# Sums of weight blocks made ahead and kept in DRAM, rotary angles on GpSimd, a scaling on ScalarE

## The chip, the cores and the metric

The kernel runs on one core of one Trainium2 chip. The time is the device time of one launch in microseconds. Engines are named as in the profile: PE (TensorE matmul), PEld (its weight load), DVE (VectorE), ACT (ScalarE), POOL (GpSimd), SP (SyncE, which here issues loads). Lines are those of the kernel before, unless "after" stands beside them.

## The reference

A trunk of two decoder layers, batch 1, 1024 tokens of width 1024, all in fp32. `cond = silu(c)`; each layer multiplies it with a 1024 x 6144 matrix and gets six vectors of shift, scale and gate.

```python
def sqrelu_mlp(h, w1, w2):                      # w1 1024 x 4096, w2 4096 x 1024
    return jnp.square(jax.nn.relu(h @ w1)) @ w2

for l in range(2):
    ada = cond @ ada_w[l] + ada_b[l]
    sh1, sc1, g1, sh2, sc2, g2 = jnp.split(ada, 6, axis=-1)
    h = modulate(rmsnorm(x, norm_g[l, 0]), sh1, sc1)
    if l == 0:
        y = mlstm_mixer(h, ...)                 # 8 heads, chunks of 128 tokens
    else:
        if shared_kv is None:                   # from x, with a modulation of its own
            shared_kv = mla_shared_kv(x, kv_shift, kv_scale, kv_norm_g, kv_w_a, ..., cos, sin)
        y = mla_mixer(h, b_w_q_a, ..., cos, sin)
    x = x + g1[:, None, :] * rmsnorm(y, norm_g[l, 1])
    h = modulate(rmsnorm(x, norm_g[l, 2]), sh2, sc2)
    y = sqrelu_mlp(h, mlp_w1[l], mlp_w2[l])
    x = x + g2[:, None, :] * rmsnorm(y, norm_g[l, 3])
```

`cos` and `sin` are the rotary tables of `positions * inv_freq`. `kv_w_a` and `b_w_q_a` are the matrices that lead to the latents of layer 1.

## The kernel before

**Matmuls.** fp32 products are made of three matmuls in a reduced format (`mm3`, L243 to L246): hi x hi, hi x lo, lo x hi. Each weight tile of 128 x 1024 is therefore loaded into one of four buffers (`raw`, by SP) and split (`wsplit`): ACT copies the high part (`wh`, L202), DVE subtracts it (`wl`, L203). There are eight such halves (`ws`). Modulation vectors are made on DVE, not on PE: eight multiply-adds per 512 columns (`ada_chunk`, L346 and L348), then four transposes on PE (L328) and a reduction (L330).

**Halves of the tokens, and the MLP.** The tokens are worked on as two halves of 512. The two halves of an MLP's up product are combined so that seven products of blocks stand for eight: `w1` is cut into 16 pairs `p_` (128 columns `p_` and 128 columns `p_ + 16`, as tiles a and b of 128 x 1024; `_l` and `_r` are the upper and lower 512 rows). `Mlp` makes three sweeps over them:
- the first (`first`, L947) multiplies a's two halves with the first token half, and POOL stores one product (`m`, L967);
- the second (`second`, L973) loads a and b, forms four block sums on DVE, o_l = b_l + b_r (L990), b_l = a_l - b_l (L991), a_l = o_l - a_l (L992), o_r = a_r - a_l (L997), splits a_l by hand (`wv`, L994 on ACT and L995 on DVE) and the tile b by `wsplit`; o is stored by POOL in `s` (L998) and partial products in `u` (L1017);
- the third (`third`, L1036) loads `s` and `u` and makes the second token half's products.

Between them the down products (`up_cols`) load `w2`, and in the first sweep POOL stores its low parts (`lo`, L1156).

**Work beside the MLP of layer 0.** `two_streams` walks the sweeps as the dense stream and takes five steps of a background (`bg_latent`) per dense step: the rest of the modulation vectors, then `rope_tables`, then `latent_weights`. `rope_tables` makes per half of the positions an angle in 128 x 512: a cast (L1263), three DVE operations (L1264 to L1266), and seven multiply-adds that take away multiples of two pi (L1268); then a clamp (L1270) and what the sine on ACT needs (L1273, L1275, L1276). `latent_weights` takes six tiles of the latents' matrices: eight multiply-adds for the shift's part (L1341, L1343), a multiplication of the whole tile with the scale (L1346, DVE, 128 x 1024), `wsplit`, and stores of both parts by POOL (`lw`, L1351 and L1353); later a transpose (L1356).

**Order.** The program is written as generators that are woven into one another (`weave`, `weave_n`, `with_bg`: so many steps of the second per step of the first) and scheduled when it is built: a planner with a timeline of its own places each instruction in its engine's queue, `tc.high_priority` and `tc.issue_after` shift it. On the chip each engine runs its queue in order and waits on semaphores. SP issues most loads in its queue's order, POOL most stores.

**The start and the mixer of layer 0.** The first 45 us transpose x and make the first modulation vectors; the last weights for them (`Piece`, L2001 to L2052) use all eight `hd` buffers (128 x 1024). Then for token half 0: `gates_in`, `qk_last`, `v_in` woven with `intra0`, `og0`; for half 1: `gates_in`, and `main` (queries, keys, values) woven with `intra0` of that half (L2294). `bgs` runs modulation chunks beside them. `k4` is a pool of 24 tiles (4 KB per partition) that the mixer and the MLP share.

Of the kernel before, what the change touches and what calls it, by code (L numbers as in the profile page):

```python
# [9 lines left out]
F32 = mybir.dt.float32  # L10
F32R = mybir.dt.float32r
# [71 lines left out]
def kernel(  # L83
# [48 lines left out]
    def raw(dt=F32):  # L132
        return sb.tile([P, 1024], dt, tag="raw", bufs=RAW, name=f"raw_{next(uid)}")
# [4 lines left out]
    def tmc(dt=F32):  # L138
        return sb.tile([P, 512], dt, tag="tmc", bufs=TMC, name=f"tmc_{next(uid)}")
# [22 lines left out]
    def scratch(shape, name):  # L162
        return dr.tile(shape, F32, tag=name, bufs=1, name=name)
# [194 lines left out]
    def ada_part(l, part):  # L358
        for j in (2 * part, 2 * part + 1):
            yield from ada_chunk(  # L360
                ada_w[l], j * 512, col(AB + l * 48 + j * 4, 4), ada[:, l, ts(j, 4)]
            )
# [553 lines left out]
                yield n7 if k == KD - 1 else n3  # L916


    NPR = DFF // P // 2
    AHEAD = 2  # L920

    class Mlp:
# [3 lines left out]
        def __init__(self, l, rows):  # L926
            self.w1, self.w2, self.rows = mlp_w1[l], mlp_w2[l], rows
            self.m = scratch([NPR, P, H], f"m{l}")
            self.u = scratch([NPR, P, 2 * H], f"u{l}")
            self.s = scratch([NPR, P, 2 * H], f"s{l}")  # L930
            self.keep = scratch([D, H], f"keep{l}")
            self.lo = scratch([4, P, DFF // P, 256], f"lo{l}")
            self.hids, self.started, self.held = ({}, {}), set(), {}
# [42 lines left out]
        def second(self, p_, ops):  # L976

            def load():  # L980
                r = [raw(), raw()]
                for i in range(2):
                    nc.sync.dma_start(
# [5 lines left out]
                l_, r_ = slice(0, 512), slice(512, 1024)  # L989
                nc.vector.tensor_add(o[:, l_], r[1][:, l_], r[1][:, r_])  # L990
                nc.vector.tensor_sub(r[1][:, l_], r[0][:, l_], r[1][:, l_])  # L991
                nc.vector.tensor_sub(r[0][:, l_], o[:, l_], r[0][:, l_])  # L992
# [33 lines left out]
        def third(self, p_, ops, buf):  # L1026


            def load():
                r, u = raw(), buf()  # L1030
                nc.sync.dma_start(r, self.s[p_])
                for i in range(2):
                    nc.sync.dma_start(u[i], self.u[p_][:, ts(i, 512)])
                return wsplit(r, 1024), u
# [216 lines left out]
    def rope_tables():  # L1251
# [7 lines left out]
        for n in range(2):  # L1259
            pi = tmc(I32)  # L1260
            nc.sync.dma_start(pi, positions[0:1, ts(n, 512)].to_broadcast([P, 512]))
            a, kf = tmc(), tmc()
            nc.vector.tensor_copy(a, pi)  # L1263
            nc.vector.tensor_scalar(a, a, inv, None, ALU.mult)  # L1264
            nc.vector.tensor_scalar(kf, a, 1.0 / (2.0 * PI), MAGIC, ALU.mult, ALU.add)
            nc.vector.tensor_scalar_add(kf, kf, -MAGIC)  # L1266
            for part in TWO_PI_PARTS:
                nc.vector.scalar_tensor_tensor(a, kf, -part, a, ALU.mult, ALU.add)  # L1268
                yield
            nc.vector.tensor_scalar(a, a, 3.1415925, -3.1415925, ALU.min, ALU.max)  # L1270
            s, t = tmc(), tmc()
# [55 lines left out]
    def latent_weights():  # L1327
# [4 lines left out]
        for b, vs in enumerate(views):  # L1332
# [7 lines left out]
            with paced():  # L1340
                nc.vector.tensor_scalar(acc, r[:, 0], sh[:, 0:1], None, ALU.mult)  # L1341
                for k in range(1, KD):
                    nc.vector.scalar_tensor_tensor(  # L1343
                        acc, r[:, k], sh[:, k : k + 1], acc, ALU.mult, ALU.add
                    )
            nc.vector.tensor_mul(r, r, A.unsqueeze(2).to_broadcast([P, KD, P]))  # L1346
            for i, t in enumerate(wsplit(r_, D)):
                if b == 2:

# [885 lines left out]
    def chain(*gs):  # L2235
        for g in gs:
            yield from g() if callable(g) else g

    bg0 = chain(*[ada_part(0, p_) for p_ in (G1, SH2, SC2, G2)])
    bg1 = chain(*[ada_kv(p_) for p_ in (0, 1)], *[ada_part(1, p_) for p_ in (SH1, SC1)])  # L2240

# [352 lines left out]
```

## Time and profile before

| what | us |
|---|---|
| median of 3 runs (lowest, highest) | 2380.63 (2376.16, 2381.13) |
| the profiled execution, whole time | 2383.9 |
| its span | 2382.1 |
| PE busy in it | 2285.4 |
| DVE busy in it | 1676.6 |
| POOL busy in it | 93.2 |

The profile is of one execution; its span runs from the first to the last recorded event, and its whole time is 1.8 us longer and 3.3 us above the median of the runs. Busy times are sums of an engine's instructions; waiting and issuing DMAs are not busy. "a <- b" behind an idle time names what ended it. The granted clock is the share of full speed at which TensorE was allowed to run. By stage, the trace has the start and the mixer of layer 0 up to about 470 us, the first sweep of its MLP to about 655, the second to about 870, and the second sweep of layer 1's MLP around 1875 to 2070.

### The profile page before, as it was taken

Reading aid. Unit: us, or ns where it says so; the run is one execution under the profiler, and the core shown is the slowest. Engines: PE = TensorE matmul, PEld = TensorE weight load, DVE = VectorE, ACT = ScalarE, POOL = GpSimd, SP = SyncE. Lnnn points to the kernel's source line nnn. Section 1 sums busy time; section 2 is a strip of 40 time slices with the busy share of each in tenths; the row PEclk is TensorE's granted clock in tenths of the full one; section 3 lists DMA queues with packets and bytes.
Section 4 is the critical chain, followed back from the end, with each engine's and each line's share of the span. In section 5 each row is a group of like instructions: output and inputs, shape, how many; then the busy total and the mean of one; then the engine's idle time right before and its main releaser. Section 6 shows DMA issues by size and latency. Waiting matters only on the chain.

```text
span 2382.1 us, 31220 instructions
## 1 busy us (share of the span) xinstructions
PE 2285.4 (96%) x11274; PEld 1886.2 (79%) x11274; DVE 1676.6 (70%) x2745; ACT 1084.1 (46%) x1811; POOL 93.2 (4%) x235
## 2 busy tenths in 40 slices
PE   8999999999898899999999989999899799999998
PEld 6888888887776788778878767878788688878887
DVE  6666767789888777767764687656638866766556
ACT  4364335674332335544444454534446233454433
POOL 1000000010011110000000000000000000000000
PEclk9999999999999999999999999999999899999999
DMA  9544454667898887655674765945256587675321
GB/s 320 162 142 118 152 155 144 196 211 250 290 295 265 282 294 252 207 191 176 203 239 159 265 218 171 327 163 184 93 149 221 157 273 228 222 252 193 115 90 70
DMA packets 402299, 482.04 MB, mean 202 GB/s; under 512 B 28419, under 2 KB 274240, under 8 KB 402144
## 3 DMA queue, kind: packets, MB, share of 16 engines
q1 hardware_dynamic: 383872, 415.44, 54.1%
q0 software_dynamic: 18272, 64.60, 7.7%
q8 instruction: 89, 1.46, 0.3%
q14 instruction: 66, 0.54, 0.1%
HBM read 358.33 MB, written 121.63 MB: 201 GB/s over the span
## 4 chain that ended last, share of the span: by engine, by line
PE 67%; issue 15%; DVE 7%; DMA 6%; ACT 2%; POOL 2%; SPq 1%; POOLq 0%; DVEq 0%; ACTq 0%
PE ps L245 11%; PE ps L244 11%; PE ps L246 11%; PE pm L244 7%; PE pm L245 7%; PE pm L246 7%; DMA raw<-in_mlp_w_dram 3%; PE pc L245 1%; PE pc L246 1%; PE pc L244 1%; DMA raw<-s 1%; PE pc L1646 1%; PE pm L791 1%; PE pm L1545 1%; DVE wl L203 1%
## 5 line engine op out<-in xcount | busy, mean ns | idle before, releaser
L202 ACT CAST wh<-raw 128x1024 fp32r<-128x1024 f32 (+4 forms) x307 | 310.6, 1015 | 508.1 <-PE pm L245 144.6
L203 DVE TENSOR_TENSOR wl<-raw,wh 128x1024 fp32r<-128x1024 f32 (+4 forms) x307 | 360.5, 1176 | 226.8 <-ACT wh L202 189.2
L244 PE MATMUL ps<-k,wh 128*128 128x512 f32 x1100 | 438.3, 399 | 8.5 <-ACT tmp L938 3.4
L245 PE MATMUL ps<-k,wh 128*128 128x512 f32 x1100 | 432.2, 393 | 2.8 <-DVE k L458 2.8
L246 PE MATMUL ps<-k,wl 128*128 128x512 f32 x1100 | 431.9, 393 | 0.8 <-DVE wl L203 0.8
L244 PEld LDWEIGHTS ps<-k,wh 128*128 128x128 f32 x1100 | 208.4, 189 | 57.2 <-ACT tmp L938 3.6
L245 PEld LDWEIGHTS ps<-k,wh 128*128 128x128 f32 x1100 | 208.6, 190 | 47.3 <-DVE k L458 4.4
L246 PEld LDWEIGHTS ps<-k,wl 128*128 128x128 f32 x1100 | 208.5, 190 | 45.6 <-DVE wl L203 1.7
L246 PE MATMUL pm<-wh,hd 128*128 128x512 f32 x488 | 191.2, 392 | 7.2 <-DVE hd L458 7.2
L244 PE MATMUL pm<-wh,hd 128*128 128x512 f32 x488 | 191.9, 393 | 1.6 <-ACT k L215 0.9
L211 DVE TENSOR_TENSOR k<-k,pm 128x512 f32<-128x512 f32 (+1 forms) x170 | 141.1, 857 | 71.8 <-PE pm L246 71.8
L245 PE MATMUL pm<-wl,hd 128*128 128x512 f32 x488 | 190.7, 391 | 0.0
L348 DVE SCALAR_TENSOR_TENSOR tma<-raw,cond,tma 128x512 f32<-128x512 f32 x168 | 125.4, 746 | 19.0 <-DMA raw<-in_ada_w_dram 10.5
L246 PEld LDWEIGHTS pm<-wh,hd 128*128 128x128 f32 x488 | 92.1, 189 | 27.4 <-DVE hd L458 8.1
L244 PEld LDWEIGHTS pm<-wh,hd 128*128 128x128 f32 x488 | 92.2, 189 | 21.8 <-ACT k L215 1.7
L245 PEld LDWEIGHTS pm<-wl,hd 128*128 128x128 f32 x488 | 92.0, 189 | 19.1 <-issue 0.2
L938 ACT ACTIVATE tmp<-tmp 128x512 f32<-128x512 f32 x80 | 50.4, 630 | 122.1 <-DVE tmp L211 102.7
L244 PE MATMUL pm<-hd,wk 128*128 128x512 f32 x256 | 101.7, 397 | 0.3 <-ACT hd L457 0.3
L244 PE MATMUL pm<-hd,wh 128*128 128x512 f32 x256 | 99.6, 390 | 1.6 <-DVE k L211 1.6
L245 PE MATMUL pm<-hd,wk 128*128 128x512 f32 x256 | 100.3, 392 | 0.6 <-DVE hd L458 0.6
L246 PE MATMUL pm<-hd,wl 128*128 128x512 f32 x256 | 99.8, 390 | 0.3 <-DVE wl L203 0.3
L246 PE MATMUL pm<-hd,wk 128*128 128x512 f32 x256 | 99.8, 390 | 0.0
(450 smaller groups left out, 4743.6 us busy)
## 6 DMA issues: line engine op xcount, KB each, us to landing
raw<-in_mlp_w_dram SPq DMA_DIRECT2D x156, 512.0 KB, 4.6
raw<-in_ada_w_dram SPq DMA_DIRECT2D x80, 512.0 KB, 4.8
raw<-in_mlp_w_dram SPq DMA_DIRECT2D x136, 256.0 KB, 4.5
raw<-in_a_w_in_dram SPq DMA_DIRECT2D x44, 512.0 KB, 4.2
lo<-wl POOLq DMA_DIRECT2D x32, 512.0 KB, 6.7
s<-k POOLq DMA_DIRECT2D x32, 512.0 KB, 4.0
u<-k POOLq DMA_DIRECT2D x32, 512.0 KB, 5.0
raw<-s SPq DMA_DIRECT2D x32, 512.0 KB, 3.6
```

Source lines behind the costliest of these rows:

```text
L202: nc.scalar.copy(hi[:, :n], r[:, :n])
L203: i = nc.vector.tensor_sub(lo[:, :n], r[:, :n], hi[:, :n].bitcast(F32))
L211: return f(*a, **k)
L244: nc.tensor.matmul(o, lh, rh, start=start, stop=False)
L245: nc.tensor.matmul(o, lh, rl, start=False, stop=False)
L246: pe_last[0] = nc.tensor.matmul(o, ll, rh, start=False, stop=stop)
L348: nc.vector.scalar_tensor_tensor(acc, r[:, kk], cond[:, k : k + 1], acc, ALU.mult, ALU.add)
L791: nc.tensor.matmul(nvs[q][:, r, i], hf.PT[p_][:, r, cs], v[2 * p_ + r], start=g == 0, stop=True,)
L938: nc.scalar.activation(s, s, AF.Relu)
L1545: nc.tensor.matmul(o[:, :w], qh, kh, start=False, stop=True)
L1646: nc.tensor.transpose(pt[:, ts(e, P)], u.prs[i][:, ts(b0 + e, P)], ident)
```

## The change

Three things change, all in layer 0 or in what runs beside its MLP.

- **Block sums.** A new generator, `block_sums`, goes over the pairs in `order` (odd ones first, then even ones, cut at 16, so all of them). Per pair POOL issues two loads of 512 KB (a and b), DVE makes the four sums in place, and POOL issues two stores of 512 KB into a new scratch in DRAM, `t0`. The first five pairs take their tiles from `hd` and run beside `gates_in` and `qk_last` of token half 0; then the tiles come from `k4`: one more pair ahead of `v_in`, and further ones at 0.2 steps per step of `main` of the second half. What is left is run to its end behind that (the `print` line). In `second`, a pair that is made loads a_l and b_l from `t0` (256 KB each), the lower half of its columns of `w1` (256 KB) and `m`, and needs no sums and no store of `s`; `third` loads its two halves from `t0`. Layer 1 keeps the old path.
- **Rotary angles.** The cast, the three operations and the seven multiply-adds move from DVE to POOL, each multiply-add as a multiplication into a third tile `d` and an addition: 18 operations per half. The clamp and what follows stay on DVE and ACT.
- **Latents' weights.** The multiplication of the tile with the scale moves from DVE (one of 128 x 1024) to ACT (eight of 128 x 128, in place).

```diff
 class Mlp:
+            self.made = not l and order or []
 def second / load():
+                if p_ in self.made:
+                    r = [raw(), raw()]
+                    nc.sync.dma_start(r[0][:, l_], t0[p_][:, 0:512])
+                    nc.sync.dma_start(r[1][:, l_], t0[p_][:, 1024:1536])
+                    nc.sync.dma_start(
+                        r[1][:, r_].rearrange("p (a b) -> p a b", b=P),
+                        wcols(self.w1, (p_ + NPR) * P, P, 4, 4),
+                    )
+                    u = k4()[:, :1024]
+                    nc.sync.dma_start(u[:, :512], self.m[p_])
+                    t = sb.tile([P, 1024], F32R, tag="ws", bufs=WS, name=f"wv_{next(uid)}")
+                    nc.scalar.copy(t[:, l_], r[0][:, l_])
+                    nc.vector.tensor_sub(t[:, r_], r[0][:, l_], t[:, l_].bitcast(F32))
+                    return (t[:, l_], t[:, r_]), wsplit(r[1], 1024), u
 def third / load():
-                nc.sync.dma_start(r, self.s[p_])
+                if p_ in self.made:
+                    nc.sync.dma_start(r[:, 0:512], t0[p_][:, 1536:2048])
+                    nc.sync.dma_start(r[:, 512:1024], t0[p_][:, 512:1024])
+                else:
+                    nc.sync.dma_start(r, self.s[p_])
 def rope_tables():
-            a, kf = tmc(), tmc()
-            nc.vector.tensor_copy(a, pi)
-            nc.vector.tensor_scalar(a, a, inv, None, ALU.mult)
-            nc.vector.tensor_scalar(kf, a, 1.0 / (2.0 * PI), MAGIC, ALU.mult, ALU.add)
-            nc.vector.tensor_scalar_add(kf, kf, -MAGIC)
+            a, kf, d = tmc(), tmc(), tmc()
+            nc.gpsimd.tensor_copy(a, pi)
+            nc.gpsimd.tensor_scalar(a, a, inv, None, ALU.mult)
+            nc.gpsimd.tensor_scalar(kf, a, 1.0 / (2.0 * PI), MAGIC, ALU.mult, ALU.add)
+            nc.gpsimd.tensor_scalar_add(kf, kf, -MAGIC)
             for part in TWO_PI_PARTS:
-                nc.vector.scalar_tensor_tensor(a, kf, -part, a, ALU.mult, ALU.add)
+                nc.gpsimd.tensor_scalar(d, kf, -part, None, ALU.mult)
+                nc.gpsimd.tensor_add(a, a, d)
                 yield
 def latent_weights():
-            nc.vector.tensor_mul(r, r, A.unsqueeze(2).to_broadcast([P, KD, P]))
+            for k in range(KD):
+                nc.scalar.activation(r[:, k], r[:, k], AF.Identity, scale=A[:, k : k + 1])
 main program
+    t0 = scratch([NPR, P, 4 * H], "t0")
+    at_prep = [k4]
+    order = [*range(1, NPR, 2), *range(0, NPR, 2)][:16]
+    def block_sums():
+        for p_ in order:
+            a, b = (at_prep[0]()[:, :1024] for _ in range(2))
+            for i, t in enumerate((a, b)):
+                nc.gpsimd.dma_start(
+                    t.rearrange("p (a b) -> p a b", b=P), wcols(mlp_w1[0], (p_ + NPR * i) * P)
+                )
+            yield
+            l_, r_ = slice(0, 512), slice(512, 1024)
+            nc.vector.tensor_add(b[:, r_], b[:, l_], b[:, r_])
+            nc.vector.tensor_sub(b[:, l_], a[:, l_], b[:, l_])
+            nc.gpsimd.dma_start(t0[p_][:, 1024:2048], b)
+            nc.vector.tensor_sub(a[:, l_], b[:, r_], a[:, l_])
+            nc.vector.tensor_sub(a[:, r_], a[:, r_], a[:, l_])
+            nc.gpsimd.dma_start(t0[p_][:, 0:1024], a)
+            yield
-    drain(with_bg(gates_in(hfs[0]), bgs, 1))
-    drain(with_bg(qk_last(hfs[0]), bgs, 1))
+    pre = block_sums()
+    at_prep[0] = hd
+    drain(with_bg(with_bg(gates_in(hfs[0]), bgs, 1), pre, 1))
+    drain(with_bg(with_bg(qk_last(hfs[0]), bgs, 1), pre, 1))
     x1 = load_x1()
+    at_prep[0] = k4
+    for _ in range(2):
+        next(pre, None)
...
-    drain(weave_n(with_bg(main, bgs, 1.5), intra0(hfs[1]), 0.95))
+    drain(weave_n(with_bg(with_bg(main, bgs, 1.5), pre, 0.2), intra0(hfs[1]), 0.95))
+    print('LEFT',len(list(pre)))
```

More of the change, by code (lines that the diff above doesn't have):

```diff
@@ L916, in residual @@
                 yield n7 if k == KD - 1 else n3
-    NPR = DFF // P // 2
     AHEAD = 2
@@ L988, in load @@
                 nc.sync.dma_start(u[:, :512], self.m[p_])
-                l_, r_ = slice(0, 512), slice(512, 1024)
                 nc.vector.tensor_add(o[:, l_], r[1][:, l_], r[1][:, r_])
@@ L2237, in chain @@
             yield from g() if callable(g) else g
+    NPR = DFF // P // 2
+    t0 = scratch([NPR, P, 4 * H], "t0")
[9 more added lines that the diff above has]
+            yield
+            l_, r_ = slice(0, 512), slice(512, 1024)
+            nc.vector.tensor_add(b[:, r_], b[:, l_], b[:, r_])
[5 more added lines that the diff above has]
+            yield
     bg0 = chain(*[ada_part(0, p_) for p_ in (G1, SH2, SC2, G2)])
```

## The prediction

> **What bounds the kernel now.** I read the page first: which engine is full, and how much of the span it is not.
>
> ```profile
> span 2382.1 us, 31220 instructions
> PE 2285.4 (96%) x11274; PEld 1886.2 (79%) x11274; DVE 1676.6 (70%) x2745; ACT 1084.1 (46%) x1811; POOL 93.2 (4%) x235
> ```
>
> PE is busy for 2285.4 of 2382.1 us, so 96.7 us of PE idleness is all that reordering can win, plus whatever the clock loses after a stall. The change removes no matmul. So I looked for where PE idles and what it waits for there. Table by stage (start:end, length, then busy time and instruction count of PE, PEld, DVE, ACT, POOL, then the granted clock, DMA share, GB/s): 540 to 660 is the end of layer 0's first up sweep, 660 to 900 its second sweep and a little more, 655 to 870 the second sweep itself, 1920 to 2040 the second sweep of layer 1.
>
> ```profile
> 540.00:600.00 60.00, 58.62 (x260) 47.48 (x259) 56.42 (x88) 28.82 (x39) 4.85 (x9) 1.00 0.73 241
> 600.00:660.00 60.00, 51.76 (x218) 41.83 (x219) 48.77 (x67) 20.66 (x26) 5.89 (x11) 0.91 0.91 306
> 660.00:720.00 60.00, 59.37 (x265) 48.50 (x264) 50.84 (x77) 20.88 (x31) 6.38 (x12) 1.00 0.93 294
> 720.00:780.00 60.00, 53.43 (x212) 42.00 (x211) 49.20 (x82) 17.59 (x24) 10.27 (x18) 0.91 0.83 259
> 780.00:840.00 60.00, 52.93 (x222) 42.10 (x222) 46.19 (x72) 19.34 (x27) 8.44 (x16) 0.94 0.88 287
> 655.00:870.00 215.00, 199.13 (x842) 160.01 (x841) 173.71 (x263) 72.88 (x102) 29.93 (x55) 0.96 0.89 283
> 1920.00:1980.00 60.00, 60.00 (x275) 49.67 (x274) 42.17 (x60) 23.45 (x33) 4.42 (x9) 1.00 0.76 244
> 1980.00:2040.00 60.00, 60.00 (x270) 49.02 (x269) 40.06 (x63) 21.37 (x30) 5.15 (x10) 1.00 0.72 229
> ```
>
> The reader is to see two things. Layer 0's second sweep loses, between 720 and 840, 6.57 + 7.07 = 13.6 us of PE time, and the granted clock of 0.91 and 0.94 costs (0.09 + 0.06) x 60 = 9.0 more: 22.6 together. The end of its first sweep loses 8.24 + 5.4 = 13.6 in 600 to 660, and 1.4 before. Layer 1's second sweep makes the same block sums and loses nothing, at a DVE load of 42 and a DMA share of 0.76.
>
> What PE waits for there: the waits of PE in 715 to 850 (three rows), DVE's longest wait in 655 to 870, and PE's longest in 540 to 720 (total us, times, longest).
>
> ```profile
> PE ps L244 <- ACT wv L994: 7.6, 3, 3.7
> PE pc L1356 <- DVE tma L1343: 3.1, 2, 2.3
> PE ps L246 <- DVE wv L995: 2.7, 3, 1.1
> DVE k L990 <- DMA raw<-in_mlp_w_dram: 28.2, 12, 6.6
> PE pc L328 <- DVE tma L348: 7.1, 2, 6.3
> ```
>
> How the first row comes about shows in DVE's timeline around PE's wait at 746, and the last row in PE's and DVE's around 606 (start, duration, idle before in brackets).
>
> ```profile
> 740.21 0.69 DVE L990 TENSOR_TENSOR k<-raw 128x512 f32<-128x512 f32 x1 [3.26 <-DMA raw<-in_mlp_w_dram]
> ...
> 742.55 0.68 DVE L992 TENSOR_TENSOR raw<-k,raw 128x512 f32<-128x512 f32 x1
> 743.15 1.22 DVE L1346 TENSOR_TENSOR raw<-raw,mods 128x1024 f32<-128x1024 f32 x1
> ...
> 746.67 0.68 DVE L995 TENSOR_TENSOR wv<-raw,wv 128x512 fp32r<-128x512 f32 x1
> 605.43 0.74 DVE L348 SCALAR_TENSOR_TENSOR tma<-raw,cond,tma 128x512 f32<-128x512 f32 x1
> 606.22 1.11 PE L328 MATMUL pc<-ident,tma 128*128 128x128 f32 x4 [6.26 <-DVE tma L348]
> ```
>
> A late load stops DVE's queue for 3.26 us; the sums that follow stand between DVE's other work, so that the pair's last half (L995) ends at 747.35, 7.1 us after the load. PE stands meanwhile. At 606 the transposes of a modulation chunk stand in PE's queue and wait for L348, the end of a DVE queue without gaps.
>
> **The change: second sweep.** Per pair, four sums leave DVE and half of the first load with the 512 KB store leaves the DMA engines (1.25 MB in and 0.5 out become 1.0 in).
>
> ```profile
> L990 DVE TENSOR_TENSOR k<-raw 128x512 f32<-128x512 f32 x32 | 22.0, 690 | 47.7 <-DMA raw<-in_mlp_w_dram 43.5 <-issue 2.4 <-DMA s<-k 1.1
> L997 DVE TENSOR_TENSOR k<-raw 128x512 f32<-128x512 f32 x32 | 21.9, 686 | 0.4
> L1346 DVE TENSOR_TENSOR raw<-raw,mods 128x1024 f32<-128x1024 f32 x6 | 7.3, 1220 | 0.1
> L215 ACT COPY v<-ps 128x128 f32<-128x128 f32 x8 | 2.2, 272 | 0.0
> ```
>
> The title says six pairs, but the list in the diff holds all sixteen, and I count sixteen. DVE loses 64 x 0.687 = 44.0 us, and 7.3 by the latents' scaling: 173.7 becomes 122.4 of 215, or 34 per 60, under layer 1's 42. The DMA engines lose 16 x 0.79 = 12.6 MB, at 283/0.89 = 318 GB/s 39.6 us, so that their share falls from 0.89 to 0.71, layer 1's. The path from load to weights becomes load, ACT copy, one DVE subtraction. The nearest stage with such loads has no stall, so I take 19 of the 22.6 us and leave 3.6 for the waits on L1343, which stay. ACT takes 48 x 0.272 = 13.1 us on top of 72.9 of 215: it has the room, but each block of eight (2.2 us) waits for DVE's reads of the same tile and stands before weight copies in ACT's queue; covered by the weights made ahead, and without that cover 6 x 2.2 = 13. Ends: -22.6 and, if the loads stay late, -5. The third sweep reads the same bytes in two loads: nothing, as SP's issues are off PE's path.
>
> **Rope tables on GpSimd.** DVE gives up 22 operations.
>
> ```profile
> L1268 DVE SCALAR_TENSOR_TENSOR tmc<-tmc,tmc 128x512 f32<-128x512 f32 x14 | 9.5, 681 | 0.0
> L1264 DVE TENSOR_SCALAR tmc<-tmc,inv 128x512 f32<-128x512 f32 x2 | 0.9, 474 | 0.0
> L1266 DVE TENSOR_SCALAR tmc<-tmc 128x512 f32<-128x512 f32 x2 | 0.8, 415 | 0.0
> L694 POOL MEMSET tmc<- 128x512 f32 x2 | 1.1, 528 | 74.6 <-PE pc L604 74.6
> masks.py:199 POOL TENSOR_SCALAR_AFFINE_SELECT ident<-ident 128x128 f32<-128x128 f32 x1 | 0.3, 336 | 0.0
> 578.49 0.42 DVE L1263 CAST tmc<-tmc 128x512 f32<-128x512 int32 x1
> ...
> 605.09 0.41 DVE L1270 TENSOR_SCALAR tmc<-tmc 128x512 f32<-128x512 f32 x1
> ```
>
> With the cast and the other addition (as L1266) that is 9.5 + 0.9 + 3 x 0.8 = 12.8 us off DVE, half of it between 578 and 605, just ahead of the 6.3 us stall. POOL has 36 operations for it. Nothing in the trace shows what one costs; by the fill it is 0.53 us, by the 128x128 selection four times over 1.34: 19 to 48 us, of which POOL has 109 of 120 free. Its clamp (L1270 before) stays on DVE and now waits for POOL, whose chain stands between the stores of m and lo; behind the clamp stand weights' L203 and L348. The second table has 26.6 us from its cast to its clamp (18 operations at up to 1.48), so a wait there is short. If POOL and DVE do not disturb each other, the stall and the half clock after it go, 6.3 + 5.4 = 11.7, up to 13 with the small ones; if each POOL operation holds DVE up for its own length, DVE carries 105.2 - 12.8 + 19 to 48 = 111 to 140 us of 120, and PE loses up to 10 and more. Between these ends I take -2, since DVE, at 56.4 of 60, has hardly a gap for POOL to work in.
>
> The Trainium skill ("SBUF — State Buffer", section "Who interferes with whom") states that a VectorE instruction with two SBUF inputs contends with a GpSimd instruction that reads SBUF, one of them blocked for the whole of the other. By that rule the term would be about +10 and the sum +1. No run here shows it so far: before, POOL has only fills, one-time masks and DMA issues.
>
> **Making the sums early.** Per pair, two loads and two stores of 512 KB, issued by POOL, and four 0.687 us sums on DVE. In all 16 x 2.1 = 33.6 MB of new traffic. Five pairs fall into the start (tiles of the modulation weights), one near 105 us, one further on, nine are written into the program behind the second half's mixer, and by the order of the changed kernel's instructions stand in DVE's queue among what ran at 347 to 423.
>
> ```profile
> 10.00:50.00 40.00, 36.55 (x228) 25.19 (x227) 28.57 (x52) 17.38 (x29) 0.45 (x5) 0.96 1.01 351
> 100.00:115.00 15.00, 15.00 (x124) 13.10 (x122) 11.32 (x20) 6.70 (x19) 0.00 (x0) 1.00 0.66 204
> 350.00:400.00 50.00, 50.00 (x276) 40.96 (x274) 30.74 (x68) 25.80 (x52) 0.10 (x1) 1.00 0.48 148
> 400.00:430.00 30.00, 30.00 (x135) 24.79 (x134) 29.29 (x41) 21.71 (x35) 0.59 (x6) 1.00 0.62 200
> 31.35 3.90 DVE L2014 SCALAR_TENSOR_TENSOR tmc<-hd,cond,tmc 128x512 f32<-128x512 f32 x5
> 36.29 1.54 DVE L2014 SCALAR_TENSOR_TENSOR tmc<-hd,cond,tmc 128x512 f32<-128x512 f32 x2 [1.04 <-DMA hd<-in_ada_w_dram]
> L998 POOL DMA_DIRECT2D s<-k x32 | 17.0, 532 | 229.3 <-DVE k L997 220.8 <-DVE tma L1343 8.3
> ```
>
> Start: the DMA engines are full (share 1.01, 351 GB/s), and DVE's wait at 36.29 is for the last modulation weights; PE's waits follow from it. POOL's first loads are released as DVE has read the tiles, from 32 on, one 0.52 MB load is 1.5 us at 351 GB/s, and two of them ahead of the two loads that count are 3 us; with the clock I take +4 (2 to 8). Near 105: DMA has a third free; +1 (0 to 3). Mixer: nine pairs need 18.9 MB, 54 us at 351 GB/s; free are 0.52 x 50 + 0.38 x 30 = 37 us, so the transfers run on past 430. The sums need 9 x 4 x 0.687 = 24.7 us; DVE has 19.3 free until 400 and 0.7 after. What overflows, 5 us, is late behind a DVE that was full, and I take that: +5. Ends: 0, if the weights made ahead cover it (PE has no idle there at all), and 15, if sums wait for late loads. POOL's issues (some 0.5 us, 64 of them) delay m's and lo's stores only if they are still queued at the first of these.
>
> **Sum**: -19 - 2 + 4 + 1 + 5 = -11 us. The profiled execution took 2383.9 for a span of 2382.1, 3.3 above the median of 2380.63; it becomes 2373, and against the median 2369.6: 2370.
>
> **Rivals.** (1) *The mixer pays* (slower). A sum whose load is late stops DVE in 370 to 430 as L990 does before in the second sweep, where one such wait took 6.6 us; behind it stand the weights' L203 and the mixer's evacuations, and PE runs dry. For: 54 us of transfers into 37 free, in a stretch in which DVE has 0.7 us to spare. Against: PE has no idle there. Nine pairs with 3 us each are 27 in place of 5: -11 + 22 = +11, 2392. It decides from 16 us of mixer stall on (11 more), where the sum is zero. (2) *POOL and DVE block each other*: sweep 1 at +10 in place of -2, sum +1, 2382. For: nearly all DVE work there reads two tiles. Against: nothing measured. (3) *The second sweep's loads stay late*: loads there come from SP's queue when tiles come free, and DVE's 28.2 us were waits for DMA, not lack of DVE time. Then only -5 of the -19 comes: sum +3, 2384. Against: layer 1's sweep with a DMA share of 0.76. (4) *Six pairs only*, as the title says: the list would have to end earlier; it does not, so it gets no chance.
>
> **How the numbers follow.** Forecast 0.50 (2358 to 2375), rival 1 0.22, rival 2 0.18, rival 3 0.10. 0.2% is 4.8 us, about what a measurement can tell from no change: faster under 2375.8, slower over 2385.4. Rival 1 is slower but for 0.03, rival 2 spreads as 0.05 faster, 0.09 same, 0.04 slower, rival 3 as 0.05 same and 0.05 slower: faster 0.55, same 0.17, slower 0.28. The range, 2352 to 2392: all gains at their best with half the costs below, rival 1 above; the forecast's own is 2358 to 2375.
>
> **What would show it.** In the second sweep: no PE wait on wv, DVE at about 34 per 60, DMA at 0.7, PE at 60. In 540 to 660: no 6 us wait of L328; the durations of L203 and L348 beside POOL's work tell rival 2. At 36 to 45 PE some us later. In 350 to 460: DVE waits at the sums' loads, and PE idle if rival 1 holds. The prediction falls if DVE's queue stands at the sums in the mixer for more than the second sweep gives back, or if the waits on wv survive.

## The result, and the profile after

The changed kernel took 2397.68 us (median of 4 runs, 2390.02 to 2399.57) beside 2379.66 before (4 runs): a ratio of 1.0072, 95% interval 1.0047 to 1.0097. It is slower by 17 us (the ratio times 2379.66). The forecast was 2370, its range 2352 to 2392. The profiled execution took 2398.78, its span is 2397.0, 14.9 longer than before.

First the top of the page after, then the stages that answer to those shown of before (start:end, length, busy time and count of PE, PEld, DVE, ACT, POOL, granted clock, DMA share, GB/s). At 690 everything runs some 35 us later than before and at 881 some 11, so 690 to 881 is the second sweep (655 to 870 before).

```profile
span 2397.0 us, 31463 instructions
PE 2285.5 (95%) x11274; PEld 1886.0 (79%) x11274; DVE 1674.5 (70%) x2717; ACT 1104.0 (46%) x1859; POOL 186.7 (8%) x319
```

```profile
10.00:50.00 40.00, 33.88 (x218) 22.89 (x216) 25.87 (x49) 14.16 (x25) 7.98 (x10) 0.93 1.07 356
60.00:80.00 20.00, 12.18 (x54) 10.31 (x53) 7.51 (x12) 5.23 (x9) 4.39 (x11) 0.78 0.97 314
350.00:400.00 50.00, 44.57 (x275) 36.73 (x274) 32.66 (x85) 16.13 (x38) 12.94 (x17) 0.93 0.75 225
400.00:460.00 60.00, 55.86 (x250) 45.26 (x249) 53.89 (x87) 30.96 (x53) 15.42 (x29) 1.00 1.05 357
540.00:600.00 60.00, 58.16 (x254) 46.91 (x253) 56.16 (x71) 32.77 (x49) 25.61 (x22) 1.00 0.63 205
600.00:660.00 60.00, 56.21 (x244) 45.31 (x243) 54.55 (x66) 23.95 (x32) 38.68 (x33) 0.97 0.83 278
690.00:881.00 191.00, 191.00 (x850) 157.86 (x849) 127.79 (x191) 91.15 (x145) 21.43 (x39) 1.00 0.78 253
```

The second sweep does what was forecast: PE is busy for 191.00 of 191 us, and the sweep that took 215 takes 191. But PE now idles more in 10 to 50, and in 60 to 80, in 350 to 400 and in 400 to 460, where it had no idle worth the name before; in 400 to 460 the DMA engines are full. POOL has twice the work.

To put the time into stages, both traces' matmuls are numbered in PE's order (11274 in both) and the starts of the same number are subtracted. The changed kernel is then late by 1.2 us at 40 us of before, 16.5 at 100, 18.3 at 140 and still at 360, 25.9 at 400, 32.3 at 460, 31.9 at 540, 35.0 at 660, 11.0 at 840, 14.8 at the end. So the start costs 18.3, the mixer of the second half 14.0 in two steps, the first sweep 2.7 (35.0 - 32.3), the second sweep gives 24.0, and 3.8 are lost further on, most of it in layer 1, where the program is not changed. Each trace is one execution, and all are set against one execution of the kernel before; from 1240 us on, in layer 1, the columns of the table below move by -3.5 to +2.5 us, so that differences of this size need not be the change's.

The waits of PE in 40 to 130, of the changed kernel (before it had two, of 0.6 and 0.3 us):

```profile
PE ps L244 <- ACT k L211: 7.8, 1, 7.8
PE pm L245 <- DVE k L461: 2.8, 1, 2.8
PE pm L244 <- ACT k L460: 2.4, 1, 2.4
```

and in 380 to 480:

```profile
PE pc L848 <- DVE tmc L822: 5.4, 1, 5.4
PE pm L244 <- ACT wh L202: 2.7, 1, 2.7
```

### The profile page after: what moved, and what is told of

It reads as the page before. It is cut to its first block, busy times and chain, and to the rows that moved or that the text cites. A ratio compares the mean times of both kernels' runs of the same rounds, so it can differ in the third digit from the quotient of the medians.

```text
span 2397.0 us, 31463 instructions
## 1 busy us (share of the span) xinstructions
PE 2285.5 (95%) x11274; PEld 1886.0 (79%) x11274; DVE 1674.5 (70%) x2717; ACT 1104.0 (46%) x1859; POOL 186.7 (8%) x319
## 4 chain that ended last, share of the span: by engine, by line
PE 56%; issue 10%; DMA 7%; DVE 7%; ACT 3%; SPq 1%; POOL 0%; DVEq 0%; POOLq 0%; ACTq 0%
PE pm L244 8%; PE pm L246 8%; PE pm L245 8%; PE ps L245 8%; PE ps L246 7%; PE ps L244 7%; DMA raw<-in_mlp_w_dram 3%; PE pc L245 2%; PE pc L246 2%; PE pc L244 2%; DVE tma L348 1%; DMA raw<-in_a_w_out_dram 1%; DVE wl L203 1%; DMA k<-in_mlp_w_dram 1%; PE pc L1666 1%
## 5 line engine op out<-in xcount | busy, mean ns | idle before, releaser
L203 DVE TENSOR_TENSOR wl<-raw,wh 128x1024 fp32r<-128x1024 f32 (+4 forms) x307 | 363.5, 1185 | 245.3 <-ACT wh L202 192.8
L244 PE MATMUL ps<-k,wh 128*128 128x512 f32 x1100 | 438.7, 399 | 13.1 <-DVE tmp L211 3.3
L211 DVE TENSOR_TENSOR k<-k,pm 128x512 f32<-128x512 f32 (+1 forms) x170 | 141.1, 858 | 83.4 <-PE pm L246 83.1
L348 DVE SCALAR_TENSOR_TENSOR tma<-raw,cond,tma 128x512 f32<-128x512 f32 x168 | 131.7, 784 | 14.0 <-DMA raw<-in_ada_w_dram 9.3
L245 PEld LDWEIGHTS pm<-wl,hd 128*128 128x128 f32 x488 | 92.2, 189 | 19.3 <-issue 0.2
L244 PE MATMUL pm<-hd,wh 128*128 128x512 f32 x256 | 99.9, 392 | 2.5 <-ACT wh L202 2.5
L245 PE MATMUL pm<-hd,wh 128*128 128x512 f32 x256 | 100.3, 392 | 1.1 <-DVE hd L458 1.1
```

Of the source, the lines that this page charges most:

```text
L203: i = nc.vector.tensor_sub(lo[:, :n], r[:, :n], hi[:, :n].bitcast(F32))
L211: return f(*a, **k)
L244: nc.tensor.matmul(o, lh, rh, start=start, stop=False)
L245: nc.tensor.matmul(o, lh, rl, start=False, stop=False)
L348: nc.vector.scalar_tensor_tensor(acc, r[:, kk], cond[:, k : k + 1], acc, ALU.mult, ALU.add)
```

## The experiments

Every run's lateness against the kernel before, by the same numbering (us; the left column is the time of the kernel before). `after` is the changed kernel; `sums_only` has the block sums alone, `rope_lat` both small moves (angles and scaling), `rope_only` the angles, `lat_only` the scaling; `traffic` the sums' transfers without the additions and `dve_sums` the additions without the transfers; `no_start` leaves out the pairs of the start, `no_start_after` also moves the later sums; `mid6` makes six pairs elsewhere, `mid6_sums` without the scaling, `mid6_late` with the sums moved. Each is taken up below.

```
before  after sums_only rope_lat rope_only lat_only traffic dve_sums no_start no_start_after   mid6 mid6_sums mid6_late
    40   +1.2      +0.3     +0.1      +0.5     +0.5    +0.4     +1.4     +0.4           +0.1   +0.4      +0.2      +0.0
   100  +16.5     +17.4     +0.1      -0.3     -1.2   +19.4     +6.5     -0.8           -1.5   -1.2      +0.2      -1.6
   140  +18.3     +20.4     +0.2      -0.3     -1.2   +20.0     +8.0     -0.5           -1.1   -1.2      +0.2      -1.6
   360  +18.3     +20.5     +0.2      -0.3     -0.4   +20.0    +12.7     -0.5           -1.1   +4.8      +7.2      +6.8
   400  +25.9     +27.5     +0.0      +0.2     -0.3   +20.7    +29.9     +7.5           +0.1   +4.9      +7.0      +7.1
   460  +32.3     +34.4     +0.0      +0.2     -0.3   +32.1    +29.9    +11.9          +13.2   +4.9      +7.0      +7.1
   540  +31.9     +34.0     +0.0      +0.2     -0.1   +32.1    +29.9    +11.6          +12.7   +4.9      +6.9      +6.9
   660  +35.0     +32.5     -0.3      +0.1     -0.1   +32.8    +28.0    +11.5          +17.2   +4.9      +7.1      +7.1
   840  +11.0      +8.7     -9.7      +3.3    -11.5   +33.1    +25.6     -7.8           -1.8  -11.0      -6.2      -8.3
  1240  +12.3     +10.0     -6.5      +3.6     -7.4   +33.6    +29.0     -5.4           -2.1   -6.9      -3.3      -5.6
  1860  +11.7      +6.0    -10.3      -0.2     -7.8   +32.8    +29.2     -5.9           -2.9  -10.8      -7.1      -6.8
  2360  +14.8     +10.9    -10.0      +0.1     -7.4   +35.2    +29.6     -7.9           -0.6  -10.4      -4.9      -4.2
```

Theory after the result: early, it is the transfers that cost, where DMA engines are full, and in the mixer the DVE sums, where they stand in a recurrence. Rivals: only the one, or only the other; and for the gain, that it belongs to the small moves and not to the sums.

**The small moves alone** (the changed kernel with an empty list of pairs).

```diff
-    order = [*range(1, NPR, 2), *range(0, NPR, 2)][:16]
+    order = []
```

> The changed kernel without its block sums: the rotary angles on GpSimd and the latents' scaling on ScalarE alone. In the changed kernel's trace GpSimd's angle operations take 55 us and DVE's operations on two tiles are longer beside them (L348 954 ns in 560 to 660 in place of 747). Theory A (GpSimd and DVE block each other, which eats the 12.8 us taken off DVE): no gain in the first sweep, DVE's L348 again over 850 ns there, a total within 5 us of before, 2377 to 2385. Rival B (the move is good, and the changed kernel's first sweep is late only because the block sums shifted it): the 6.3 us wait of the transposes for L348 and the half clock after it go, 8 to 12 us faster, 2368 to 2372. On both the start and the mixer stay as before; of the second sweep's 22.6 us most stays lost.

Measured: 2372.34 beside 2383.59, ratio 0.9951 (0.9936 to 0.9966). Faster. The first sweep gave nothing (-0.3 at 660), as theory A has it; the whole gain, 9.4 us, lies in the second sweep, where I had expected most of the loss to stay. The total is therefore outside theory A's range, and near rival B's for another reason than B's. For 9.4 of its 24 us the second sweep does not need the block sums taken away.

**The sums alone** (rotary angles and latents' scaling as before).

> The changed kernel with the rotary angles and the latents' scaling back on DVE: the block sums alone. The changed kernel lost 18.3 us in 40 to 130, 14 in 368 to 440, 3 in 540 to 655 and won 24 in the second sweep. If these are the sums' own: 18 + 14 - 24 (+-3), first sweep at 0, 2386 to 2392. If the latents' move carries part of the second sweep's gain (7.3 us less on DVE): the gain there falls under 18, 2393 or more.

Measured: 2395.41 beside 2383.59, ratio 1.0050 (1.0033 to 1.0067); 20.4 lost by 140, 13.9 in the mixer, 23.8 won between 660 and 840. The total is above the 2386 to 2392 that was expected; the kernel before was itself at 2383.59 beside it. So the sums carry both the losses and, without the small moves, nearly the same gain: what the two would win in the second sweep is the same 24 us, and either takes a part of it.

**Transfers and DVE's sums apart.** Both runs use the old path in both MLPs, with angles and scaling as before, so nothing can be won. The first keeps loads and stores and leaves the four additions out; the second keeps the additions on tiles filled with zeros and leaves the transfers out.

```diff
 first, second:
-            self.made = not l and order or []
+            self.made = []
 first:
-            nc.vector.tensor_add(b[:, r_], b[:, l_], b[:, r_])
-            nc.vector.tensor_sub(b[:, l_], a[:, l_], b[:, l_])
-            nc.vector.tensor_sub(a[:, l_], b[:, r_], a[:, l_])
-            nc.vector.tensor_sub(a[:, r_], a[:, r_], a[:, l_])
 second:
-            for i, t in enumerate((a, b)):
-                nc.gpsimd.dma_start(...)
+            nc.gpsimd.memset(a, 0.0)
+            nc.gpsimd.memset(b, 0.0)
-            nc.gpsimd.dma_start(t0[p_][:, 1024:2048], b)
-            nc.gpsimd.dma_start(t0[p_][:, 0:1024], a)
```

> The kernel before with the 32 loads and 32 stores of 512 KB of the block sums at their places, but without the four DVE sums, and both MLPs on the old path (so what is stored is not used). Theory T (the loss at the start and in the mixer is that of transfers on full DMA engines): 15 to 18 us lost in 40 to 130, 8 to 14 in 360 to 440, total 2403 to 2413. Rival S (it is DVE's queue that stands at the sums): under 5 us at the start and under 4 in the mixer, total 2381 to 2389.

> The kernel before with the 64 DVE sums of the block sums at their places, on tiles that GpSimd fills with zeros in place of loading them, no stores, both MLPs on the old path. Theory T (transfers): at most 5 us in all, 2380 to 2385, since DVE has room up to 400 us and the start has waits for DMA. Rival S (sums on DVE): 10 us and more at the start, 8 and more in 360 to 440, total over 2398.

Measured: transfers alone 2419.05 beside 2383.59, ratio 1.0150 (1.0135 to 1.0165); additions alone 2414.22, ratio 1.0123 (1.0107 to 1.0140). The first total is above theory T's range, the second within rival S's, and neither theory holds everywhere. The transfers cost 20.0 at the start, nothing at 360 to 400 (0.7) and 11.4 after 400. The additions cost 8.0 at the start, 4.7 and then 17.2 up to 400, and nothing after. So each of the mixer's two steps has a cause of its own, and both can cost at the start.

*The start.* It has two steps. The changed kernel is 1.2 us late at 42 us of before, 5.5 from 50 to 62, 14.6 at 65 and 16.5 at 100. The additions alone make the first step (1.4, then 5.4 up to 65) and not the second; the transfers alone make the second (-1.2 at 62, 18.0 at 65) and not the first.

First step, DVE in the changed kernel:

```profile
44.10 0.69 DVE L2274 TENSOR_TENSOR hd<-hd 128x512 f32<-128x512 f32 x1 [2.10 <-DMA hd<-in_mlp_w_dram]
...
46.58 0.15 DVE L2059 TENSOR_TENSOR ada<-pc,cols 128x4 f32<-128x4 f32 x1
49.12 0.69 DVE L2274 TENSOR_TENSOR hd<-hd 128x512 f32<-128x512 f32 x1 [1.79 <-DMA hd<-in_mlp_w_dram]
```

A sum (L2274 after) stands in DVE's queue and waits for its load. Behind the first of them L2059, which ACT's L460 needs, runs at 46.58 in place of 43.69 (L2039 before), and PE waits 2.4 us for L460; behind the second stands L461, for which PE waits 2.8.

Second step. Three loads of SP's bring the next projection's weights, two of 408 KB and one of 272. How long they took to land (KB each, median us), of the kernel before (37 to 50 us) and, below, of the changed kernel (45 to 58), with the two queues' share of the packets' time in 40 to 80 (q0 is POOL's, q1 SP's):

```profile
raw<-in_a_w_in_dram SPq DMA_DIRECT2D x2, 408.0 KB, 7.9
raw<-in_a_w_in_dram SPq DMA_DIRECT2D x1, 272.0 KB, 2.8
```

```profile
q0 software_dynamic: 2260, 8.21, 58.9%
q1 hardware_dynamic: 3473, 5.30, 41.3%
hd<-in_mlp_w_dram POOLq DMA_DIRECT2D x6, 512.0 KB, 10.4
raw<-in_a_w_in_dram SPq DMA_DIRECT2D x2, 408.0 KB, 22.9
raw<-in_a_w_in_dram SPq DMA_DIRECT2D x1, 272.0 KB, 19.0
```

SP's weights took 19 to 23 us in place of 3 to 8. With the additions alone, without POOL's transfers, they took 6.6 and 2.8, so it is the transfers in POOL's queue, more than half of full engines, that made them late. ACT's copies of these weights wait for them, and PE for ACT, 7.82 us in the changed kernel and 17.95 with the transfers alone. In the changed kernel:

```profile
67.95 0.88 ACT L202 CAST wh<-raw 128x816 fp32r<-128x816 f32 x1 [12.58 <-DMA raw<-in_a_w_in_dram]
72.87 0.87 ACT L202 CAST wh<-raw 128x816 fp32r<-128x816 f32 x1 [4.04 <-DMA raw<-in_a_w_in_dram]
76.78 0.60 PE L244 MATMUL ps<-wh,k 128*128 128x272 f32 x1 [7.82 <-ACT k L211]
```

PE's wait is named after ACT's evacuation, the last of several; what arrived late was the weights. Part of the rest is the clock, 0.78 of full speed in 60 to 80. The Trainium skill ("DMA: Bandwidth & Descriptors", section "Queues, rings and completion order") says that each DMA engine takes turns between the queue rows that have work. That both queues moved packets in the same 40 us, 58.9 to 41.3, agrees with that.

*The mixer, first step.* One link of the chunks' recurrence runs on DVE from L813 to L822, behind which PE's L848 waits. DVE's timeline of the kernel before, in the link at which the changed kernel's PE waits (start, duration):

```profile
361.76 0.15 DVE L813 TENSOR_SCALAR sm<-pm 128x4 f32<-128x4 f32 x1
...
362.02 0.68 DVE L818 TENSOR_REDUCE sm<-tmc 128x4 f32<-128x512 f32 x1
...
365.99 0.16 DVE L417 SCALAR_TENSOR_TENSOR sm<-sm,sm 128x4 f32<-128x4 f32 x1
366.19 0.69 DVE L822 TENSOR_TENSOR tmc<-pm,sm 128x512 f32<-128x512 f32 x1
```

the same link with the additions alone (L2270 to L2273 are the four sums), and what PE waited for there in 360 to 400:

```profile
384.72 0.16 DVE L813 TENSOR_SCALAR sm<-pm 128x4 f32<-128x4 f32 x1
384.79 1.28 DVE L2270 TENSOR_TENSOR k<-k 128x512 f32<-128x512 f32 x2
...
386.06 0.68 DVE L818 TENSOR_REDUCE sm<-tmc 128x4 f32<-128x512 f32 x1
386.66 1.28 DVE L2271 TENSOR_TENSOR k<-k,k 128x512 f32<-128x512 f32 x2
...
394.37 0.68 DVE L822 TENSOR_TENSOR tmc<-pm,sm 128x512 f32<-128x512 f32 x1
PE pc L848 <- DVE tmc L822: 17.2, 3, 9.8
```

and the end of the same link in the changed kernel, where it began at 381.64, with DVE's wait for the sums' loads in 360 to 460:

```profile
389.31 0.69 DVE L2274 TENSOR_TENSOR k<-k 128x512 f32<-128x512 f32 x1 [1.55 <-DMA k<-in_mlp_w_dram]
389.91 0.68 DVE L822 TENSOR_TENSOR tmc<-pm,sm 128x512 f32<-128x512 f32 x1
DVE k L2274 <- DMA k<-in_mlp_w_dram: 4.6, 4, 2.4
```

From L813 to the end of L822 it took 5.1 us before, 10.3 with the additions alone and 9.0 in the changed kernel; the link ahead of it went from 3.7 to 15.0 and 7.2. Most steps of a link are 0.16 us with gaps of a few hundredths between them (before, a split, L203, and two updates, L841, already stand in this one); with the additions alone one or two sums of 0.69 us stand in nearly every gap, and PE waits for the end of the link. In the changed kernel the loads hold sums back (10 of the mixer's 40 had run by the end of this link, with the additions alone 39), so that its step is smaller (7.6). But one sum with a late load stands in front of L822 itself, and 1.55 us of the link are that wait.

*The mixer, second step.* In 425 to 475 of the changed kernel ACT waited for the output projection's weights:

```profile
ACT wh L202 <- DMA raw<-in_a_w_out_dram: 9.3, 1, 9.3
```

**Without the start's pairs, and then with the sums behind the recurrence.** The first leaves pairs 1, 3, 5, 7, 9 on the old path. The second also queues the sums that are left on DVE behind the last L822 of the second half's chunks (`scaled` records that instruction), while the loads may go early.

```diff
 both:
-    order = [*range(1, NPR, 2), *range(0, NPR, 2)][:16]
+    order = [*range(1, NPR, 2), *range(0, NPR, 2)][5:]
-    drain(with_bg(with_bg(gates_in(hfs[0]), bgs, 1), pre, 1))
-    drain(with_bg(with_bg(qk_last(hfs[0]), bgs, 1), pre, 1))
+    drain(with_bg(gates_in(hfs[0]), bgs, 1))
+    drain(with_bg(qk_last(hfs[0]), bgs, 1))
 second:
+            with tc.issue_after(gate_[0]) if gate_[0] else nullcontext():
+                nc.vector.tensor_add(b[:, r_], b[:, l_], b[:, r_])
...
-    print('LEFT',len(list(pre)))
     in_turn(
         wout(a_w_out[0], hfs[0].o, lambda m, pt: evac(y0[m], pt)), chunks0(hfs[1]), iter(())
     )
+    gate_[0] = scaled[0].ins
+    drain(pre)
```

> The changed kernel without the five pairs that are made in the first 100 us; these five take the old path in the second and third sweep, the other eleven stay where they were. If the start's 18.3 us are all those pairs' doing: nothing lost in 40 to 100 (up to 2 near 110 by the pair there), the mixer's 14 as before, and the second sweep still gains most of its 24: total 2374 to 2382, 16 to 20 under the changed kernel. If the second sweep's gain is in proportion to the pairs (11 of 16 of 24 is 16.5, 7.5 less), 2384 to 2390.

> The run without the pairs of the start, with the sums that were left queued on DVE behind the second half's last output scaling; their loads stay early. That run lost 8.0 us at 360 to 380 and 4.0 at 430 to 440. Theory R: the step at 360 to 380 falls under 2 us, the step after 420 grows, as stores come later into full DMA engines: 5 to 12. Rival T (transfers make both steps): 360 to 380 still loses 5 or more.

Measured: 2374.96 beside 2381.07, ratio 0.9971 (0.9953 to 0.9989), and 2382.03 beside 2381.03, ratio 1.0002 (0.9990 to 1.0014). Without the start's pairs nothing is lost by 140, the mixer's 8.0 and 4.4 stay, and the second sweep still gives 19.3 of 24 with eleven of sixteen pairs. With the sums behind the recurrence the first step is gone (1.2 up to 400), which is what theory R forecast; the second grows to 13.1, just above the 12 that I had allowed, and the sum over both is no better. The loss moved with the work: the sums now stand among the splits of the mixer's output (L761, L765), and PE waits 4.0 us for one of these (L765) and 3.9 for ACT (L646). Its first sweep lost another 4.5 us (12.7 to 17.2), whose cause stays open.

**Six pairs at a quieter place.** Pairs 1 to 11 (odd) while the first half's chunks run, where DMA had 0.2 to 0.5 of its time taken: with the scaling on ScalarE, with the scaling as before, and with the sums queued behind the last L822 of these chunks (`side` takes a step of each generator in turn; `held` keeps the loaded pairs). The start's and the second half's pairs are gone. The angles stay on DVE in all three.

```diff
-    order = [*range(1, NPR, 2), *range(0, NPR, 2)][:16]
+    order = [*range(1, NPR, 2), *range(0, NPR, 2)][:6]
...
-    in_turn(og0(hfs[0], hdv), chunks0(hfs[0]), n1)
+    in_turn(og0(hfs[0], hdv), chunks0(hfs[0]), side(n1, pre))
...
 third of them only:
+    last_ = scaled[0].ins
     drain(n1)
+    for q in held:
+        with tc.issue_after(last_):
+            drain(sums(*q))
```

> Six pairs (1, 3, 5, 7, 9, 11) made while the first half's chunks run (140 to 240 us, DMA share 0.2 to 0.5, DVE 5 to 8 of 10 us), one step per step of the chunks; latents' scaling on ScalarE, the angles on DVE. If wide sums cost by standing in a recurrence of small DVE steps, and transfers only on full DMA engines: at most 5 us there, as the output gates' matmuls run beside; second sweep -15 to -24: total 2358 to 2371. If the sums cost 2 us per pair wherever they stand: 12 lost, total 2370 to 2378.

> The same six pairs at the same place with the latents' scaling on DVE as before: what the sums alone bring there. If the second sweep's loss needs the late loads and DVE's four sums in the stretch of the latents: pairs 5 to 11 lie there, -10 to -20 in the second sweep, total 2363 to 2375. If six of sixteen bring only their share of 24, 9: 2371 to 2378.

> The run with six pairs in the first half's chunk stage, with one thing moved: the 24 sums are queued on DVE behind the last output scaling of the chunks (L822), with their stores, while the loads stay where they were. That run lost 6.0 us at 190 to 220. Theory R (a wide sum costs where it stands between the small steps of the chunks' recurrence, which PE waits for): under 2 us lost at 190 to 240; total 2364 to 2370. Rival T (it is the loads and stores there): 4 to 6 us lost all the same. Rival D (DVE's time is the price, wherever the sums stand): the loss moves to 220 to 300, 4 us or more.

Measured: 2373.75 (0.9968, 0.9955 to 0.9981), 2375.61 (0.9979, 0.9969 to 0.9988), both beside 2381.07, and 2376.36 beside 2381.03 (0.9979, 0.9968 to 0.9990). I had hoped for less: the place costs 6.0 to 7.0 us, for these chunks are the same recurrence. In the first of these runs three links in a row, 5.8, 3.2 and 5.1 us long before, took 9.6, 8.2 and 11.0. All three totals lie above the range of the theory that the run was to test. Moved behind it, the step at 190 to 220 is gone, but 8.9 us are lost at 260 to 280, by a wait of 5.0 us for a weight tile and the clock after it (0.83 in 260 to 280). That tile's load was issued at 269.3 us, 5.5 later than before (263.8), when DVE released it, and DVE's own operations ran as much later (L676 at 250.3 in place of 244.6), though PE was 2 us early until then. Rival D, that DVE's time is the price wherever the sums stand, fits this run better than R. The six sums alone still win 13.3 us in the second sweep.

**Each small move alone.** An empty list of pairs, and one of the two moves undone.

```diff
-    order = [*range(1, NPR, 2), *range(0, NPR, 2)][:16]
+    order = []
 scaling alone:
-                nc.gpsimd.tensor_scalar(d, kf, -part, None, ALU.mult)
-                nc.gpsimd.tensor_add(a, a, d)
+                nc.vector.scalar_tensor_tensor(a, kf, -part, a, ALU.mult, ALU.add)
...
 angles alone:
-            for k in range(KD):
-                nc.scalar.activation(r[:, k], r[:, k], AF.Identity, scale=A[:, k : k + 1])
+            nc.vector.tensor_mul(r, r, A.unsqueeze(2).to_broadcast([P, KD, P]))
```

> The kernel before with the latents' scaling on ScalarE alone. The run with this and the rotary angles on GpSimd won 9.7 us, all of it in the second sweep (655 to 830), and nothing in the first. If the gain is the scaling's: 7 to 11 us faster, 2369 to 2374 beside 2380. If it came from the angles, which finish the background's earlier steps sooner or later: under 3 us.

> The kernel before with the rotary angles on GpSimd alone. Theory A (GpSimd's operations hold up DVE's on two tiles for as long as the 12.8 us that it was relieved of): within 3 us of before up to 660, L348 over 850 ns in 540 to 660, nothing won in the second sweep: total 2377 to 2384. Rival B (the angles' move carries a part of the 10 us of the two small moves together): 2371 to 2376.

Measured: the scaling alone 2371.45 beside 2381.07, ratio 0.9961 (0.9948 to 0.9974); the angles alone 2384.14 beside 2380.39, ratio 1.0022 (1.0010 to 1.0033). The scaling on ScalarE alone beats both kernels of this case (both small moves together, 0.9951, lie within its interval's reach and can't be told from it). Its 11.4 us in the second sweep come from moving six DVE operations of 1.22 us to ScalarE; 4.1 are lost again between 840 and 1240. The second sweep and PE's waits there, with the scaling alone:

```profile
655.00:870.00 215.00, 205.45 (x893) 166.17 (x892) 175.78 (x270) 97.81 (x158) 31.67 (x62) 0.99 0.91 295
PE ps L244 <- ACT wv L1008: 4.0, 4, 1.7
PE pc L1375 <- DVE tma L1361: 1.9, 1, 1.9
```

PE is busy for 6.3 us more of the same stretch and the clock is 0.99 in place of 0.96; the longest wait is 1.9 us in place of 3.7. Whether the shorter waits are the reason for the clock, no run here takes apart.

The angles: DVE's groups in 540 to 660 before, and then with the angles alone on GpSimd (count, busy, mean ns), followed there by two groups of GpSimd's own in 500 to 700, and last the stages of that run.

```profile
L348 DVE SCALAR_TENSOR_TENSOR tma<-raw,cond,tma 128x512 f32<-128x512 f32 x41 | 30.6, 746 | 2.9 <-DMA raw<-in_ada_w_dram 2.5
L203 DVE TENSOR_TENSOR wl<-raw,wh 128x1024 fp32r<-128x1024 f32 x19 | 23.2, 1219 | 7.8 <-ACT wh L202 7.7
L211 DVE TENSOR_TENSOR tmp<-tmp,ps 128x512 f32<-128x512 f32 x9 | 6.1, 678 | 0.8 <-PE ps L246 0.8
L346 DVE TENSOR_SCALAR tma<-raw,cond 128x512 f32<-128x512 f32 x5 | 2.4, 475 | 0.0
```

```profile
L348 DVE SCALAR_TENSOR_TENSOR tma<-raw,cond,tma 128x512 f32<-128x512 f32 x41 | 37.2, 908 | 2.9 <-DMA raw<-in_ada_w_dram 2.3
L203 DVE TENSOR_TENSOR wl<-raw,wh 128x1024 fp32r<-128x1024 f32 x18 | 24.5, 1363 | 4.0 <-ACT wh L202 4.0
L211 DVE TENSOR_TENSOR tmp<-tmp,ps 128x512 f32<-128x512 f32 x9 | 6.1, 677 | 0.0
L346 DVE TENSOR_SCALAR tma<-raw,cond 128x512 f32<-128x512 f32 x5 | 4.2, 850 | 0.0
L1286 POOL TENSOR_SCALAR tmc<-tmc 128x512 f32<-128x512 f32 x14 | 24.4, 1740 | 2.1 <-DVE k L458 1.0
L1287 POOL TENSOR_TENSOR tmc<-tmc,tmc 128x512 f32<-128x512 f32 x14 | 19.6, 1398 | 0.7
```

```profile
540.00:600.00 60.00, 56.23 (x247) 44.99 (x246) 55.94 (x66) 27.43 (x38) 39.89 (x33) 1.00 0.71 237
600.00:660.00 60.00, 53.91 (x234) 43.41 (x233) 53.02 (x65) 21.75 (x27) 26.83 (x24) 0.97 0.89 296
```

DVE was relieved of 12.8 us, yet its busy time went from 105.2 (56.42 + 48.77) to 109.0 (55.94 + 53.02): what was left of it, 92.4, grew by 16.6 us, beside 55.4 us of GpSimd's operations on the angles (estimated at 19 to 48). L348, with two tiles in SBUF, grew from 746 to 908 ns on average; L211, which reads one operand from PSUM, did not move (678 and 677). The Trainium skill ("SBUF — State Buffer", section "Who interferes with whom") states that the first kind contends with a GpSimd instruction that reads SBUF and that a DVE instruction with at most one SBUF input outside the two-port modes does not. These rows agree; L346 with one SBUF input went from 475 to 850, which agrees with the page only if it ran in such a mode; that it took 475 ns before, where an operation with two tiles of the same shape took 690 (L990), speaks for one, but no row names it.

## Why the prediction was wrong, point by point

- **What bounds the kernel, and the second sweep** (-19, ends -22.6 and -5): right, and more than taken: -24.0, nearly all that the sweep lost in 655 to 870 before (15.9 us of PE time, and 0.04 x 215 = 8.6 by the clock). PE has no wait there. DVE's work in the sweep is 127.8 us, near the forecast's 122.4; it is 40 per 60 rather than 34, and DMA's share 0.78 rather than 0.71, because the sweep takes 191 us and the forecast divided by the old 215. ACT's scaling cost 403 ns an operation, 18.8 us in all, where 272 and 13.1 were taken from a copy, and PE did not wait for it. What I got wrong is the account: I gave the gain to the sums' 44 us and put the scaling's 7.3 us in with it. The scaling alone gives 11.4 of it, and the angles with the scaling 9.4. Whether the rest comes from DVE's sums or from the transfers saved there, no run separates.
- **"With the clock I take +4 (2 to 8)"**, the start: this step failed; with the pair near 105 (+1) it measured 18.3. The wait that it priced did not come: SP had issued all the modulation weights by 28, POOL's first load followed at 33.7, and the last of the weights landed at 37.9 in place of 37.5. Two others came that the sum did not have. Sums standing at their loads in DVE's queue cost 4.3 (1.2 to 5.5). The ten loads and ten stores are 10.5 MB, 29 us at 356 GB/s, and compete with what SP loads until they are done: the next projection's weights were late by 9.1 more, and the clock and the pair near 105 make up the rest. Transfers alone lose 20.0 by 140, the additions alone 8.0.
- **"DVE has 19.3 free until 400 and 0.7 after; what overflows, 5 us, is late"**, the mixer: this step failed too. It measured 14.0, inside the ends of 0 and 15 but far from the value. The free time was not free: part of it is the gaps of a recurrence, and a sum that stands in a gap lengthens the recurrence (7.6; with the additions alone 17.2). The transfers that "run on past 430" cost a further 6.4 (alone 11.4), where the output projection's weights arrive late. Ten pairs stand there, not nine: the one "further on" runs at 369 to 373.
- **The rotary angles** (-2, ends -13 and +10): in the changed kernel the first sweep lost 2.7; alone the angles lose 0.1 to 660 and 3.3 to 840, and 3.8 over the whole run (2384.14 for 2380.39). Rival 2's mechanism is there, at a third of its price. My bounds for GpSimd's operations were too low: 1.40 and 1.74 us against 0.53 and 1.34.
- **Rival 1** (the mixer pays, from 16 us more) named the right side, 2392 against 2397.68. Its mechanism is in the traces, DVE standing at a sum whose load is late: 4.6 us in the mixer, and 3.9 at the start, for which the rival was not written. But its condition was not met (14.0 us of mixer stall where it needed 16), and the start, which had no rival, added the other 13. That its total lies so near is partly luck.
- **Six pairs only** got no chance and has none: sixteen pairs are made, and the title above does not say six.
- The 3.8 us lost after 840 were no term of mine. 1.3 of them fall before 1240, where most of the runs lose 1 to 4 us, those that won in the second sweep (4.1 with the scaling alone) and `dve_sums`, which did not (3.4); why, stays open. The other 2.5 lie within what layer 1 shows from trace to trace.

## What to carry to other kernels

Idle time of an engine inside a recurrence is latency of the chain: count the links and what an inserted operation adds to each, not the sum of the gaps. Moving the sums behind the recurrence did not help here either: the loss moved with them (13.1 and 8.9 us). Transfers prefetched into a stage with full DMA engines made loads land late that were issued well after them (19 to 23 us in place of 3 to 8), so price all of their bytes at the full rate, not the two transfers next to the critical one. And before work is moved far away, try the small relief in the stage itself: taking six operations off DVE's queue gave here what 33.6 MB of new traffic could not keep.

## What the runs showed of the hardware

GpSimd's multiplication by a constant with one operation took 1740 ns on 128x512 on average (L1286, with the angles alone), longer than its addition of two tiles (1398), while a multiplication with an addition in one instruction (L1283, the same shape, two of them) took 632, all beside a busy DVE:

```profile
L1283 POOL TENSOR_SCALAR tmc<-tmc 128x512 f32<-128x512 f32 x2 | 1.3, 632 | 0.2
```

I had expected the form with less to do to be the cheaper one; the cause stays open.
